# Five small rearrangements in a one-core hybrid encoder block: sums with fewer products, a later scaling, two earlier low parts, a later and cheaper norm

## The chip, the cores and the metric

The kernel runs on one core of one Trainium2 chip. The metric is the device time of one execution in microseconds, taken as the median of three runs of the kernel before; the same kernel was also profiled once, and the profile's rows come from that execution.

## What is computed

The reference is one layer of a residual block over 512 tokens of width 1024. Cut to what matters here:

```python
h = rmsnorm(x); z = h @ W_in                    # 416 latent columns, then diff q, k, v (3 x 512)
x = x + concat([mla(z), diff(z)], -1) @ W_out   # 8 MLA heads of 64, 4 differential heads of 128
h2 = rmsnorm(x)
x = x + (silu(conv3(h2 @ W_gate)) * (h2 @ W_up)) @ W_down      # 2816 wide
x = x + sigmoid(rmsnorm(x) @ W_pg) * (p @ W_pp)

def diff(...):   # per head: two softmaxes, their difference times V, then
    return rms_norm(o, out_g) * (1 - lam_init)
```

So there are three norms of `x` over its 1024 features, and each differential head's output has a norm of its own.

## The kernel before, in words

Everything is float32. Each large product is made of three passes, `mm3` (lines 152 to 157): both operands are split into a high part (rounded to the type `fp32r`, a copy on ScalarE) and a low part (the remainder, a subtraction on VectorE), and TensorE multiplies high by high (L155), high by low (L156) and low by high (L157). So every weight costs a copy on ScalarE and a subtraction on VectorE before its products, and so does every activation. Helpers that do this are `load_w` (L143), `split` (L180), `hi_`, `lo_` and `hl` (L822 to L832).

TensorE holds `x` transposed: 128 features on the partitions, 512 tokens along the free axis, eight such blocks (`xb(b)`). Sums over the features for a norm run over partitions, so TensorE makes them with a matrix of ones.

The order of TensorE's work is written out by hand for the whole kernel. The order of VectorE, ScalarE and GpSimd is written by hand in two stretches (from the start up to the fifth step of the MLA heads, and from the output projection's last part through the first gate and up products); between and behind them the framework's planner draws it up. `tc.issue_after(x)` adds an edge: the instructions in its block are queued behind `x` on the engine of `x`. A tile has a tag, and tiles of one tag share a number of buffers (`bufs`); a load or a copy into a tile waits until its buffer is free.

The parts that the change touches, in order of time:

1. **First norm (L275 to L360).** ScalarE squares the four raw input tiles (two feature blocks of 512 tokens each, side by side), VectorE adds the four into `xq[:, 0]`, 1024 wide (L210, L278). While the latent products `zA` run (`mm3` of 416 columns, four token tiles `t` for each pair of feature blocks `kq`), TensorE sums `xq` over the partitions: for each of four token tiles two products with one column of ones, one for each half of the 1024 (L359). `rms` (L159) turns the sums into `rx`: one VectorE operation and a power on GpSimd (L163). `rx` scales the latent outputs `za` (L367).
2. **MLA heads and the output projection's weights.** `slots` steps through 8 heads by 4 token tiles. The first 512 rows of `w_out` come in four tiles `o00` to `o03` through `load_w`, called when `wo_units` (L638) is first pumped, behind the last MLA step; the three raw buffers and five pairs of high and low buffers are shared with the weights before. `last_mla` (L717) makes, in the last head's steps, the transposes of the finished outputs: `y_split` 0, 1 and 2; `y_split` 3 follows behind the first two steps of the differential heads' logits.
3. **Differential heads (L768 to L786).** `dslots` steps through 4 heads by 4 token tiles; a step makes the logits two steps ahead, pumps units of the output projection (`o`, each ended by VectorE's `add_x`, L631), transposes probabilities, and multiplies by V for the step before (`diff_pv`, L685). At a head's last tile `diff_pv` also makes the output's norm: squares and a copy on ScalarE (L696, L697), a reduction and two small operations on VectorE (L699 to L703), the power on GpSimd (L704), and the scaling of the copy by it on VectorE (L706, 128x512). That call stands in step t = 0 of the next head. Its output is transposed and split in step t = 2 of the next head (`y_split(4 + h - 1)`, L780).
4. **Second norm and the embedding's product (L1008 to L1027).** `norm_r` (L910) sums `nrm["ss"]` with four one-column products, makes the power and spreads it over a diagonal on VectorE (L917); `norm_b` (L919) multiplies ones by that diagonal, and ScalarE copies the result to `nrm["r"]`, 128x512 (L922). `pp_unit(b)`, b = 0 to 7, is one block of the product `p @ W_pp` (six passes, filler for TensorE), `pp_out(b)` its copy on ScalarE into one of three `t5` buffers and its write to DRAM. `tokens` (L978) makes the normed, split inputs `b1` and `b2` of the gate and up products, on VectorE and ScalarE, one block per `next(tk)`.
5. **Gate and up products, first part (L1160 to L1260).** Written out by hand on all engines: three plain products, then products of halves (`gu_units`), with `w_steps` and `token_sums` on VectorE and ScalarE between. `d0 = down_hi(0)` copies the high part of the first down weight, `up_split(2, cv2)` splits the third block's output, `dn0 = [lo_(*d0)]` makes that weight's low part.
6. **Third norm (L1340 to L1350).** After the first half (k = 0 to 3) of the first two blocks of the product `pg`, `norm_r` runs; after the second half `norm_b`. `ple_out` (L1330) multiplies each block by `nrm["r"]` (L1334), which frees its PSUM bank; blocks 0 to 3 use the four banks that blocks 4 to 7 use again.

`rms_v` (L165) is the power by VectorE alone: a first guess from the bits, then three Newton steps, eleven operations in all.

Of the kernel before, what the change touches and what calls it, by code (L numbers as in the profile page):

```python
# [94 lines left out]
def hybrid_block(ctx: ExitStack, tc: tile.TileContext, a: dict, out: bass.AP):  # L95
# [66 lines left out]
        V.tensor_scalar(m, ss, 1.0 / width, EPS, op0=ALU.mult, op1=ALU.add)  # L162
        G.tensor_tensor(y, m, mhalf[:, :n], op=ALU.pow)  # L163

    def rms_v(y, ss, n, width):  # L165

        m, g, t = (sm.tile([P, 32], F32, tag=f"rs_{i}", name=f"rs_{i}")[:, :n] for i in ("n", "g", "t"))
        V.tensor_scalar(m, ss, 1.0 / width, EPS, op0=ALU.mult, op1=ALU.add)
        V.tensor_scalar(y.bitcast(I32), m.bitcast(I32), -0.5, 0x5F3759DF, op0=ALU.mult, op1=ALU.add)
        V.tensor_tensor(g, y, m, op=ALU.mult)  # L170
        for i in range(3):
            V.scalar_tensor_tensor(t, g, -0.5, y, op0=ALU.mult, op1=ALU.mult)
            V.scalar_tensor_tensor(y, t, 1.5, y, op0=ALU.add, op1=ALU.mult)
            if i < 2:
                V.scalar_tensor_tensor(g, t, 1.5, g, op0=ALU.add, op1=ALU.mult)
# [100 lines left out]
    nc.sync.dma_start(mk[QK:100, :], a["maskk"])  # L276
    squares(3)
    V.tensor_tensor(xq[:, 0], xq[:, 0], xq[:, 2], op=ALU.add)  # L278


    rc, rs = {}, {}
# [65 lines left out]
    for kq in range(4):  # L347
        if kq == 0:
            for j in range(2):
                for t in range(NT):  # L350
                    mm3(zps[t][:, :416], xblocks(0, 2, t, *wa[0], 416)[j:j + 1], j == 0, False)
        for t in range(NT):
            if kq:
                mm3(zps[t][:, :416], xblocks(2 * kq, 2 * kq + 2, t, *wa[kq], 416), False, kq == 3)
            if (kq, t) == (2, NT - 1):
                sps = bank("ob", "ssx")
                for u in range(NT):
                    for j in range(2):
                        TE.matmul(sps[:, u:u + 1], xq[:, 0, j * T + u * P:j * T + u * P + P], ones[:, :1], start=j == 0, stop=j == 1)  # L359
                rms(rx, sps[:, :NT], NT, D)  # L360


# [245 lines left out]
        strips.append(strip)  # L608


    yh, yl = [None] * 8, [None] * 8

    def y_split(i, src, col, tag):

        ps = bank(tag, f"yT{i}")
        for t in range(NT):
            TE.transpose(ps[:, tsl[t]], src[:, tsl[t]], ident)
        yh[i], yl[i] = th_tile(f"yh{i}")
        split(yh[i], yl[i], ps, col)

    def wo_blocks(k0, k1, b, w):

# [7 lines left out]
    def add_x(b, ps):  # L630
        V.tensor_tensor(xb(b), xb(b), ps, op=ALU.add)  # L631

    wo2 = {}

    def wo_w(kq, dq):
        return load_w(a["w_out"][kq, dq], 1024, f"o{kq}{dq}")

    def wo_units(kq, dqs, nk):  # L638

        for dq in dqs:  # L640
# [3 lines left out]
            for b in (2 * dq, 2 * dq + 1):  # L644
                ps = bank("acc", f"o{kq}{b}")
                for k in range(0, nk, 2):
# [1 line left out]
                    if k == nk - 2:  # L648
                        add_x(b, ps)
                    yield  # L650

    df = {}

    def diff_T(h, c):
        ps = bank("tp" if h else "acc", f"d{c}T{h}")
        for t in range(NT):
            TE.transpose(ps[:, tsl[t]], zd[c][t][:, h * P:(h + 1) * P], ident)
        h_, l_ = st[4 * (h % 2) + 2 * c], st[4 * (h % 2) + 2 * c + 1]
        split(h_, l_, ps, dcol if c == 0 else None)
        df["qk", h, c] = (h_, l_)  # L660
# [24 lines left out]
    def diff_pv(h, t):  # L685
        if t == 0:
            df["po"] = bank("ob", f"do{h}")
        po, pt = df["po"], df.pop(("pt", h, t))
        for j in range(t + 1):
            TE.matmul(po[:, tsl[t]], pt[:, tsl[j]], zd[2][j][:, h * P:(h + 1) * P], start=j == 0, stop=j == t)  # L690
        if t < NT - 1:
            return
        s0 = df["s0", h]
        yn = tt(f"yd{h}")
        sq = sq_tile("sqo")[:, :T]
        S.activation(sq, po, AF.Square)  # L696
        df["copy"] = S.copy(yn, po)  # L697
        sso = sm.tile([P, NT], F32, tag="sso", name="sso")
        V.reduce_sum(sso, sq.rearrange("p (t d) -> p t d", d=P), axis=AX.X)  # L699

        mo, ro = sm.tile([P, NT], F32, tag="mo", name="mo"), sm.tile([P, NT], F32, tag="ro", name="ro")
        V.scalar_tensor_tensor(mo, s0, EPS, s0, op0=ALU.mult, op1=ALU.mult)
        V.scalar_tensor_tensor(mo, sso, 1.0 / P, mo, op0=ALU.mult, op1=ALU.add)  # L703
        G.tensor_tensor(ro, mo, mhalf[:, :NT], op=ALU.pow)  # L704
        yv = yn.rearrange("p (t d) -> p t d", d=P)
        df["scale"] = V.tensor_tensor(yv, yv, ro.unsqueeze(2).broadcast_to([P, NT, P]), op=ALU.mult)  # L706
        df["y", h] = yn

    dslots = [(h, t) for h in range(DH) for t in range(NT)]
    x_sb = []  # L710
# [19 lines left out]
    for i, (h, t) in enumerate(slots):  # L730
        if i < 2:
            (mla_q, mla_k)[t](1)
        if i + 1 < len(slots):
            mla_logits(*slots[i + 1])
        if i == 4:
            region.__exit__(None, None, None)
            held = tc.issue_after(mla["nm"].ins)
            held.__enter__()
        if i == 8:
            held.__exit__(None, None, None)  # L740
            with tc.issue_after(mla["k"].ins):
                zd_norm(0)
        if 0 < h < H - 1 and t < 2:
            (mla_q, mla_k)[t](h + 1)
        if i == 1:
            lo(*z1_hi(3))
        if i in (9, 11, 13, 15):
            with tc.issue_after(mla["nm"].ins):
                zw2.append(load_w(a["w_d"][2, len(zw2)], 1024, f"d2{len(zw2)}"))
        if h < H - 1:  # L750
            pump(FILL_MLA[t])
        if i == 6:
            bias_strip()
        if h == H - 1:
            if t == 0:
                pump(100)
                fill.append(wo_units(0, range(4), 4))
            last_mla[t]()
        mla["pt", h, t] = probs_T(mla.pop(("pm", h, t)), t, f"m{h}{t}", t % 2)
        if i:  # L760
            mla_pv(*slots[i - 1])
# [6 lines left out]
    for i, (h, t) in enumerate(dslots):  # L768
        if i + 2 < len(dslots):
            diff_logits(*dslots[i + 2])  # L770
        pump(FILL_DIFF[h][t])
        df["pt", h, t] = probs_T(df.pop(("pm", h, t)), t, f"d{h}{t}", True)
        if i:
            diff_pv(*dslots[i - 1])
        if h + 1 < DH and t == 0:
            diff_T(h + 1, 0)
        if t == 3 and h + 2 < DH:
            diff_T(h + 2, 1)
        if h and t == 2:
            y_split(4 + h - 1, df["y", h - 1], ocol, "tp")  # L780
        if h and t == 3:
            if h == 2:
                fill.append(wo_units(1, range(2), 2))
# [223 lines left out]

    tk, w1 = tokens(), w_plain(1)  # L1008
    s0 = hi_(raw_w(gu(0, 2, 4), "rS", 0, bufs=3), "wS", 0)
    for b in range(2):  # L1010
        pp_unit(b)
    norm_r()
    for b in range(2):
        pp_out(b)
    for b in range(2, 4):
        pp_unit(b)
    W[0][1] = lo_(*s0)
    pp_out(2)
# [2 lines left out]
    next(tk)  # L1021
    pp_out(3)
    for b in range(4, 8):
        pp_unit(b)
        next(tk)
        pp_out(b)
    for _ in tk:  # L1027
# [184 lines left out]
    up_mul(cv2, u2, 1.0)  # L1212
    next(new)
    next(g)
    up_split(2, cv2)
    dn0 = [lo_(*d0)]
    w5 = w_steps(5)
    old, g = g, new
    next(g)
# [121 lines left out]
    for k in (0, 4):  # L1341
        for b in range(2):
            pg(b, ps[b], k, k + 4)
        if k == 0:
            norm_r()
    norm_b()
    pg(2, ps[2])
    for b in range(2):
        ple_out(b, ps[b])
# [91 lines left out]
```

## Time and profile before

| | us |
|---|---|
| runs of the kernel before | 655.7, 655.98, 654.2 |
| median | 655.7 |
| profiled execution, its own time | 653.42 |
| its span, first to last instruction | 651.6 |
| TensorE busy in it | 641.6 |
| VectorE busy | 475.2 |
| ScalarE busy | 362.9 |
| GpSimd busy | 56.6 |

The granted TensorE clock was 1.0 throughout. The profiled execution has 1.8 us outside its span, and is 2.3 us below the median. An "idle before" in a timeline row, in brackets, is the time the engine stood still before that instruction and what ended it; the chain of waits is followed back from the last instruction.

### The profile page before, as it was taken

The numbers are of one execution on the slowest core, as the hardware profiler recorded it, in microseconds if no ns is written. First come the engines' busy times: TensorE is split into PE (matmuls) and PEld (weight loads), VectorE is DVE, ScalarE is ACT, GpSimd is POOL, SyncE is SP. The second block draws the span as 40 slices with busy tenths as digits, with TensorE's granted clock in tenths as the row PEclk, the third lists the DMA queues.
The fourth block names the chain that finished last, engine by engine and source line by source line (L and its number), as shares of the span: only waits on it lengthen the run. The fifth ranks groups of instructions, "written<-read, shape, count | busy, mean of one in ns | idle before, by whom it ended". The sixth has DMA issues, their size and how long they took to land.

```text
span 651.6 us, 10276 instructions
## 1 busy us (share of the span) xinstructions
PE 641.6 (98%) x3932; PEld 569.5 (87%) x3932; DVE 475.2 (73%) x860; ACT 362.9 (56%) x631; POOL 56.6 (9%) x93
## 2 busy tenths in 40 slices
PE   9999999999999999999999999999999999999997
PEld 9988888888777778889999999999999999988886
DVE  6789587656878677888886767677767676759444
ACT  7797666457666455556554555455454545637211
POOL 1520040000000121000100000000010000000000
PEclk9999999999999999999999999999999999999999
DMA  8241235234100248636675646565646453531121
GB/s 303 96 162 40 91 73 171 66 115 144 33 33 2 64 179 254 162 70 178 174 215 127 179 114 181 122 197 116 179 114 177 116 176 114 179 130 60 38 80 49
DMA packets 29912, 82.63 MB, mean 127 GB/s; under 512 B 3100, under 2 KB 4124, under 8 KB 29736
## 3 DMA queue, kind: packets, MB, share of 16 engines
q1 hardware_dynamic: 23816, 69.17, 31.9%
q0 software_dynamic: 5616, 12.33, 11.1%
q8 instruction: 31, 0.51, 0.3%
q10 hardware_dynamic: 432, 0.49, 0.2%
q14 instruction: 17, 0.14, 0.1%
HBM read 77.77 MB, written 5.52 MB: 128 GB/s over the span
## 4 chain that ended last, share of the span: by engine, by line
PE 88%; DVE 7%; ACT 3%; issue 1%; DMA 1%; POOL 0%; ACTq 0%; DVEq 0%; POOLq 0%
PE dn L157 6%; PE dn L156 6%; PE dn L155 6%; PE gx L157 4%; PE gx L155 4%; PE gx L156 4%; PE g L155 4%; PE g L156 4%; PE g L157 4%; PE zd L155 3%; PE zd L157 3%; PE zd L156 3%; PE pg L155 2%; PE pg L157 2%; PE pg L156 2%; PE u L155 2%
## 5 line engine op out<-in xcount | busy, mean ns | idle before, releaser
L828 DVE TENSOR_TENSOR wSl<-rS,wSh 128x1024 fp32r<-128x1024 f32 x21 | 25.7, 1224 | 44.5 <-ACT wSh L824 44.4
L157 PE MATMUL dn<-ah,lo_dn 128*128 128x512 f32 x144 | 56.4, 392 | 0.0
L156 PE MATMUL dn<-al,hi_dn 128*128 128x512 f32 x144 | 56.3, 391 | 0.0
L155 PE MATMUL dn<-ah,hi_dn 128*128 128x512 f32 x144 | 56.0, 389 | 0.0
L945 POOL DMA_DIRECT2D rS<-in_w_gu x19 | 22.7, 1195 | 250.9 <-DVE cv L1112 115.0
L824 ACT CAST wSh<-rS 128x1024 fp32r<-128x1024 f32 x21 | 22.1, 1051 | 35.8 <-PE gy L156 35.5
L155 PE MATMUL zd<-hi_d,xh 128*128 128x512 f32 x96 | 39.4, 410 | 0.0
L156 PE MATMUL zd<-lo_d,xh 128*128 128x512 f32 x96 | 37.5, 391 | 0.0
L631 DVE TENSOR_TENSOR x<-x,dn 128x512 f32<-128x512 f32 x44 | 29.8, 678 | 6.5 <-PE dn L157 6.3
L828 DVE TENSOR_TENSOR wTl<-rA,wTh 128x1024 fp32r<-128x1024 f32 x19 | 23.3, 1224 | 14.9 <-ACT wTh L824 14.3
L573 ACT ACTIVATE pm<-ml,nm,rq 128x128 f32<-128x128 f32 (+3 forms) x32 | 19.7, 617 | 22.7 <-DVE nm L571 22.7
L157 PEld LDWEIGHTS dn<-ah,lo_dn 128*128 128x128 f32 x144 | 27.0, 187 | 5.7
L155 PEld LDWEIGHTS dn<-ah,hi_dn 128*128 128x128 f32 x144 | 27.1, 188 | 5.2
L156 PEld LDWEIGHTS dn<-al,hi_dn 128*128 128x128 f32 x144 | 27.0, 188 | 5.3
L155 PE MATMUL o<-yh,hi_o 128*128 128x512 f32 x64 | 26.9, 420 | 1.0 <-DVE x L631 1.0
L1115 ACT ACTIVATE cv<-cv 128x512 f32<-128x512 f32 x22 | 13.9, 631 | 24.5 <-DVE cv L1112 24.4
L824 ACT CAST wAh<-rA 128x1024 fp32r<-128x1024 f32 x21 | 22.0, 1050 | 9.1 <-DMA rA<-in_w_gu 9.1
L570 DVE TENSOR_REDUCE nm<-ml 128x1 f32<-128x128 f32 (+3 forms) x32 | 15.6, 486 | 15.3 <-PE ml L157 15.3
L155 PE MATMUL g<-b2h,wAh 128*128 128x256 f32 (+1 forms) x88 | 26.3, 299 | 0.1
L676 ACT ACTIVATE pmd<-pmd,nmd 128x128 f32<-128x128 f32 (+3 forms) x32 | 17.9, 560 | 15.1 <-DVE nmd L675 15.1
L156 PE MATMUL g<-b2l,wAh 128*128 128x256 f32 (+1 forms) x88 | 26.2, 297 | 0.0
L157 PE MATMUL g<-b2h,wAl 128*128 128x256 f32 (+1 forms) x88 | 26.2, 297 | 0.0
(467 smaller groups left out, 2226.8 us busy)
## 6 DMA issues: line engine op xcount, KB each, us to landing
rA<-in_w_gu SPq DMA_DIRECT2D x22, 512.0 KB, 3.9
rS<-in_w_gu SPq DMA_DIRECT2D x22, 512.0 KB, 3.5
rS<-in_w_gu POOLq DMA_DIRECT2D x19, 512.0 KB, 6.0
raw_dn<-in_w_down SPq DMA_DIRECT2D x18, 512.0 KB, 5.9
raw_d<-in_w_d SPq DMA_DIRECT2D x12, 512.0 KB, 3.7
r<-in_w_gu SPq DMA_DIRECT2D x19, 256.0 KB, 6.5
raw_o<-in_w_out SPq DMA_DIRECT2D x8, 512.0 KB, 3.7
rS_pg<-in_w_pg SPq DMA_DIRECT2D x6, 512.0 KB, 3.9
```

Of the source, the lines that this page charges most:

```text
L155: TE.matmul(ps, xh, wh, start=first and i == 0, stop=False, skip_group_check=again)
L156: TE.matmul(ps, xh, wl, start=False, stop=False, skip_group_check=again)
L157: TE.matmul(ps, xl, wh, start=False, stop=last and i == n - 1, skip_group_check=again)
L570: V.reduce_max(nm, ps[:, :n], axis=AX.X, negate=True)
L573: S.activation(pm[:, :n], ps[:, :n], AF.Exp, bias=nm, scale=r, accum_out=mla["ssum", h // 2][:, t, h % 2:h % 2 + 1])
L631: V.tensor_tensor(xb(b), xb(b), ps, op=ALU.add)
L676: S.activation(pm[:, :n], pm[:, :n], AF.Exp, bias=nm, scale=-1.0, accum_out=s0 if m == 0 else s1)
L824: S.copy(h_, src)
L828: V.tensor_tensor(l_, src, _f32(h_), op=ALU.subtract)
L945: nc.gpsimd.dma_start(sums[f].rearrange("p (i c) -> p i c", i=2), a["w_gu"][f][:, :2048].rearrange("p (i c) -> p i c", i=2)[:, :, :512], a ...
L1115: S.activation(cv, cv, AF.Silu)
```

## The change

The edits: in the first norm the two halves of `xq` are added on VectorE and the sums take four products, one position later; a differential head's scaling (not the last head's) is issued in step t = 1 of the next head; the first output weight is loaded beside the last MLA step, and its low part is queued behind the low part of the third `y_split`; three `pp_unit`s stand ahead of `norm_r` and one more ahead of `norm_b`; the first down weight's low part stands ahead of `up_split(2)`; and the third norm is one product of a matrix of ones with `nrm["ss"]` (128x512) and `rms_v` on all 512 columns, in place of `norm_r` and `norm_b`, its scratch in tiles that are free there.

```diff
-    def rms_v(y, ss, n, width):
-
-        m, g, t = (sm.tile([P, 32], F32, tag=f"rs_{i}", name=f"rs_{i}")[:, :n] for i in ("n", "g", "t"))
+    def rms_v(y, ss, n, width, room=None):
+
+        m, g, t = room or (sm.tile([P, 32], F32, tag=f"rs_{i}", name=f"rs_{i}")[:, :n] for i in ("n", "g", "t"))
...
     V.tensor_tensor(xq[:, 0], xq[:, 0], xq[:, 2], op=ALU.add)
+    V.tensor_tensor(xq[:, 0, :T], xq[:, 0, :T], xq[:, 0, T:], op=ALU.add)
...
-            if (kq, t) == (2, NT - 1):
+            if (kq, t) == (3, 0):
                 sps = bank("ob", "ssx")
                 for u in range(NT):
-                    for j in range(2):
-                        TE.matmul(sps[:, u:u + 1], xq[:, 0, j * T + u * P:j * T + u * P + P], ones[:, :1], start=j == 0, stop=j == 1)
+                    TE.matmul(sps[:, u:u + 1], xq[:, 0, tsl[u]], ones[:, :1], start=True, stop=True)
                 rms(rx, sps[:, :NT], NT, D)
...
-        split(yh[i], yl[i], ps, col)
+        df["ysplit"] = split(yh[i], yl[i], ps, col)
...
-    wo2 = {}
+    wo2, wo_first = {}, {}
 
     def wo_w(kq, dq):
+        if (kq, dq) in wo_first:
+            return wo_first.pop((kq, dq))
         return load_w(a["w_out"][kq, dq], 1024, f"o{kq}{dq}")
...
         yv = yn.rearrange("p (t d) -> p t d", d=P)
-        df["scale"] = V.tensor_tensor(yv, yv, ro.unsqueeze(2).broadcast_to([P, NT, P]), op=ALU.mult)
         df["y", h] = yn
+        df["scaling"] = lambda: V.tensor_tensor(yv, yv, ro.unsqueeze(2).broadcast_to([P, NT, P]), op=ALU.mult)
+        if h == DH - 1:
+            df["scale"] = df["scaling"]()
...
             last_mla[t]()
+            if t == NT - 1:
+                raw = load_raw(a["w_out"][0, 0], 1024, "o00")
+                hi_o, lo_o = (wts.tile([P, 1024], F32R, tag=i, bufs=NW, name=f"{i}_o00") for i in ("hi", "lo"))
+                S.copy(hi_o, raw)
+                with tc.issue_after(df["ysplit"].ins):
+                    V.tensor_tensor(lo_o, raw, _f32(hi_o), op=ALU.subtract)
+                wo_first[0, 0] = (hi_o, lo_o)
...
+        if h and t == 1:
+            df["scaling"]()
...
-    for b in range(2):
+    for b in range(3):
         pp_unit(b)
     norm_r()
     for b in range(2):
         pp_out(b)
-    for b in range(2, 4):
+    for b in range(3, 5):
         pp_unit(b)
...
     for b in range(4, 8):
-        pp_unit(b)
+        if b < 7:
+            pp_unit(b + 1)
         next(tk)
         pp_out(b)
...
+    dn0 = [lo_(*d0)]
     up_split(2, cv2)
-    dn0 = [lo_(*d0)]
...
         if k == 0:
-            norm_r()
-    norm_b()
+            sps = bank("ob", "nr3")
+            TE.matmul(sps, ones, nrm["ss"], start=True, stop=True)
+            rms_v(nrm["r"], sps, T, D, (nrm["dg"], nr_[1][:, T:], nrm["ss"]))
```

More of the change, by code (lines that the diff above doesn't have):

```diff
@@ L608, in bias_strip @@
         strips.append(strip)
-    yh, yl = [None] * 8, [None] * 8
+    yh, yl, df = [None] * 8, [None] * 8, {}
     def y_split(i, src, col, tag):
@@ L650, in wo_units @@
                     yield
-    df = {}
     def diff_T(h, c):
```

## The prediction, made before the changed kernel ran

> **What bounds the kernel now.** I read the page first, then the chain of waits, then the view of who waited for whom on TensorE, and last the timeline around each wait.
>
> ```profile
> PE 641.6 (98%) x3932; PEld 569.5 (87%) x3932; DVE 475.2 (73%) x860; ACT 362.9 (56%) x631; POOL 56.6 (9%) x93
> PE 88%; DVE 7%; ACT 3%; issue 1%; DMA 1%; POOL 0%; ACTq 0%; DVEq 0%; POOLq 0%
> L155 PE MATMUL o<-yh,hi_o 128*128 128x512 f32 x64 | 26.9, 420 | 1.0 <-DVE x L631 1.0
> ```
>
> TensorE is busy for 98% of the span and carries 88% of the chain. Time can be won in two ways only: TensorE does less, or one of its few waits goes. Those of more than a moment, apart from the start's, are these (us in total, times, longest):
>
> ```profile
> PE pTm L538 <- ACT pm L573: 1.1, 2, 0.9
> PE o L155 <- DVE x L631: 1.0, 1, 1.0
> PE gx L157 <- DVE wAl L828: 0.6, 1, 0.6
> PE kT L557 <- DVE st L187: 0.5, 2, 0.2
> PE dl L157 <- DVE st L187: 0.4, 1, 0.4
> PE nr L914 <- DVE nr L886: 0.4, 1, 0.4
> ```
>
> They add to 4.0 us. A record of a 512-column product is about 0.42 long (row above) and the next starts 0.23 later (607.88 row below), so records overlap by some 0.16 and a wait behind such a product costs TensorE up to 0.16 more than its row.
>
> **Products that go.**
>
> ```profile
> 20.27 1.68 PE ssx L359 x16
> 606.75 0.79 PE nr L914 x8
> 607.54 0.35 PE pg L155
> 607.88 0.23 PE pg L156
> 613.14 0.86 PE nrb L921 x2
> ```
>
> The first norm's eight one-column products show as 16 passes in 1.68 us, 0.105 each; four products go, 8 passes, **0.84 us** off TensorE's path. Before them VectorE gets one more addition of 128x512; the next fence has one at 0.69. Two things cover it: the sums now stand six 416-column products later, and if that were too little, what is left of the 0.69 would fall on TensorE.
>
> At the third norm the eight passes take 0.79, and the product behind them 0.35 in place of 0.23: 0.91 us. The spreading product, 0.86, stays in another form: ones by `ss`, again 512 float32 columns. So **0.91 us** goes. The power and the diagonal give way to eleven VectorE operations of 512 columns. No such chain is in the trace; its nearest row is a 128x512 operation on two tensors:
>
> ```profile
> 614.66 0.69 DVE L1334 TENSOR_TENSOR sg<-pg,nr 128x512 f32<-128x512 f32 x1 [5.08 <-ACT nr L922]
> 624.96 0.69 DVE L1334 TENSOR_TENSOR sg<-pg,nr 128x512 f32<-128x512 f32 x1 [1.50 <-PE pg L157]
> ```
>
> Eleven by 0.69 is 7.6 us. They start at the end of the new product, about 606.75 + 0.86 = 607.6, and end at about 615.2; the first user is at 614.66 now. So the first `ple_out` runs half a microsecond later. Who waits: block 4's product, which takes block 0's bank. Blocks 2 and 3 still lie ahead of it, 48 passes of 0.23 from 614.0 on, so it starts at 625.0 now and at 624.1 then. The cover is over 8 us, and I cost the eleven operations at nothing; they fall on the path only if they take twice their estimate.
>
> **The first output weight's low part.** The MLA heads hold one wait on VectorE that comes from it:
>
> ```profile
> 115.26 1.14 DVE lo_o L149
> 119.13 0.67 DVE st L187
> ```
>
> The low part of `o00` ran at 115.26, though its first use is behind the MLA heads; the split `st` ended 0.05 before `kT` (the row `PE kT`) could start. Without 1.14 ahead of it that wait goes: half of the row's 0.5, plus the overlap, **0.4 us**. No other low part can move into its place, since the next needs a pair of buffers that the differential values' weights still hold. The load on SyncE's queue and the high part keep their places, as far as buffers decide; the raw buffer is held some 45 us longer, so the later loads of `w_out` make do with two, each still issued a low part ahead of the one that uses it.
>
> Now the low part runs behind the third output's:
>
> ```profile
> 161.52 0.29 DVE L675 CUSTOM_DVE_ANT_0 pmd<-dl,strip 128x128 f32<-128x128 f32 x1 [0.43 <-PE dl L157]
> 162.47 0.69 DVE L588 TENSOR_TENSOR ym<-mo,rcp 128x512 f32<-128x512 f32 x1 [0.44 <-PE mo L583]
> 166.74 0.61 DVE yh3l L184
> 167.40 0.50 PE o L156
> ```
>
> VectorE stands still there for 0.43 and 0.44, which takes in 0.87 of 1.14. The rest, 0.27, is queued ahead of the fourth output's low part, and the product at 167.40 starts 0.05 after that ends: bounds 0 and 0.35; I take **0.2 us lost**, near the rest.
>
> **The heads' scaling.**
>
> ```profile
> 201.34 1.01 POOL L704 TENSOR_TENSOR ro<-mo,mhalf 128x4 f32<-128x4 f32 x1 [14.57 <-DVE mo L703]
> 201.79 0.61 DVE L682 SCALAR_TENSOR_TENSOR pmd<-pmd,cf 128x384 f32<-128x384 f32 x1
> 202.38 0.69 DVE L706 TENSOR_TENSOR yd<-yd,ro 128x512 f32<-128x512 f32 x1
> 214.49 0.62 DVE pmd L682
> 216.52 1.02 POOL ro L704
> 217.56 0.69 DVE L706 TENSOR_TENSOR yd<-yd,ro 128x512 f32<-128x512 f32 x1 [0.58 <-POOL ro L704]
> 218.26 0.61 DVE x L631
> 218.91 0.50 PE o L155
> ```
>
> Before the last head's step VectorE stands for 0.58 until the power ends at 217.54, scales, and only then adds the `x` whose bank TensorE waits for: the 1.0 row. With the scaling a step later the addition can start at 217.0, 1.2 us sooner, which is more than the wait: **1.1 us** with the overlap. In the head before, the scaling at 202.38 stands directly ahead of the split that `dl` waits for: 0.69 sooner ends the whole wait, **0.45 us**. The scaling costs the same wherever it runs; its user is the transpose in step 2, a step of TensorE work behind, so I cost its new place at nothing.
>
> A rule of the Trainium skill speaks against this (SBUF — State Buffer, section Who interferes with whom): a VectorE instruction with two inputs in SBUF contends with a GpSimd instruction that reads SBUF, and the second to start stands still until the first ends. By it VectorE, freed of its wait, would stand still anyway under the power. The rows do not bear it out: the combination at 201.79 began 0.45 into the power and took 0.61, as the same one at 214.49 did with no power beside it (0.62).
>
> **The second norm, and what happens to its gain.** With `pp_unit(2)`, six passes, ahead of `norm_r` the `nr` wait of 0.4 (0.5 with the overlap) goes. But the norm then starts when those passes end, 6 by 0.23 less the 0.5 later: about 0.85. TensorE has won 0.5, and the chain from the norm to `tokens` is 0.85 late. Is there slack?
>
> ```profile
> 248.00:258.60 10.60, 10.60 (x47) 8.40 (x46) 8.79 (x14) 5.75 (x11) 0.00 (x0) 1.00 1.02 306
> 258.68 0.59 ACT L937 COPY ppo<-pp 128x512 f32<-128x512 f32 x1 [0.80 <-DMA pps<-ppo]
> DVE wTl L828 <- ACT wTh L824: 2.0, 2, 1.7
> DVE wSl L828 <- ACT wSh L824: 1.1, 1, 1.1
> DVE b2l L987 <- ACT b2h L989: 0.5, 1, 0.5
> DVE wAl L828 <- ACT wAh L824: 0.5, 1, 0.5
> ```
>
> The last four rows are all waits of VectorE from 259 to 291.7, where `gx` waits for `wAl`. None is ended by TensorE: VectorE and ScalarE hand each other casts and low parts all the way from the `ppo` copy at 258.68, which a DMA released. So the time at 291 is set by that DMA, not by TensorE, and the 0.5 won is waited away there. The DMA is in a stretch where the engines are full (share 1.02, 306 GB/s): it starts up to 0.85 later but carries one 256 KB write less, since `ppo` 2 now goes out before it, worth 0.86 at that rate. Bounds 0 and 0.85 late; nearest to 0 by the rate, I take 0.2 **lost**.
>
> The first down weight's low part then acts on the next wait of the same chain:
>
> ```profile
> 301.18 0.69 DVE L184 TENSOR_TENSOR al<-cv,ah 128x512 fp32r<-128x512 f32 x1 [1.02 <-ACT ah L183]
> 301.79 1.22 DVE L828 TENSOR_TENSOR lo_dn<-raw_dn,hi_dn 128x1024 fp32r<-128x1024 f32 x1
> 301.35 1.04 ACT L824 CAST wAh<-rA 128x1024 fp32r<-128x1024 f32 x1
> ```
>
> VectorE idles 1.02 before `al`. Put there, `lo_dn` delays `al` by 0.2, and `wAl`, which ran behind `lo_dn`, starts when its high part ends, at 302.4 instead of about 302.9 (`lo_dn` ends at 303.0 and records overlap a little here too): `gx` gets **0.5 us** back. Together 0.3 won.
>
> **The sum.** 0.84 + 0.91 + 0.4 - 0.2 + 1.1 + 0.45 + 0.3 = 3.8 us. The profiled execution took 653.42 (span 651.6, 1.8 around it); it would take 649.6. The median of the runs is 2.3 above it; taken from that, 655.7 - 3.8 = **651.9 us**, 0.6% less. Of this, 1.75 are passes that are gone and need no wait to vanish.
>
> **The rivals.**
>
> *The scaling keeps its place.* VectorE's order there is the planner's. If it deals the scaling as soon as it counts the power as done, it stands ahead of the addition as now, or so late that the transpose waits 0.7 for it. For: the planner put it there before, idle time and all. Against: its place in the program is now behind that addition. The 1.55 are lost: 653.4. By the Trainium skill's rule the time would be this too, the 1.55 being stood out under the power.
>
> *The chain pays in full.* The write does not shorten the full stretch: 0.85 late instead of 0.2, so 652.5. For: `ppo` 3 to 5 are also issued later. Against: the rate.
>
> *A new dealing of low parts: slower.* One row shows what a low part in the wrong place does:
>
> ```profile
> 155.52 1.21 DVE L149 TENSOR_TENSOR lo_o<-raw_o,hi_o 128x1024 fp32r<-128x1024 f32 x1
> ```
>
> It ran just ahead of the last small step of a row maximum; the exponential followed, and `pTm` waited 0.9 (1.07 with the overlap). A moved step lets the planner deal VectorE's list anew from the MLA heads on. Twelve low parts lie there, and two cost TensorE something now. From the fourth more in such a place on, the kernel is slower; five give 5 x 1.07 - 3.8 = +1.5, 657.2. Against: the edits there are small and late.
>
> **How the numbers follow.** Forecast 0.60; scaling keeps its place 0.17; the Trainium skill's rule 0.03; the chain pays in full 0.13; new dealing 0.07. A measurement of this kernel tells about 0.3%, 2.0 us, from no change. The forecast and the chain rival lie beyond it nearly always, 0.72; the two cases at 653.4 in six of ten, 0.12: faster 0.84. Of the rest, 0.08 from those and 0.03 of the others fall within: same 0.11. Slower 0.05. The low end adds what could go beyond: the 0.2 of the MLA heads, and in the second norm's chain the 0.5 kept, the 0.2 not lost and the last 0.1 of the `gx` row, 1.0 in all, and half a microsecond because the runs of before spread over 1.8: 650.4. The high end is the scaling rival with the chain paid in full, 0.65 more, and a little of the `yh3l` bound: 654.2.
>
> **What would show it.** Right: L359 with 8 passes at 0.84 and no `nr` passes near 607; no wait `o <- x` over 0.3 and none of `dl` on `st`; L706 in the second and third head behind an addition, with no idle before it; the wait `nr <- nr` gone, `gx` waiting longer at 291 and less at 303; eleven operations of 0.7 near 608 with TensorE not waiting behind them. Wrong: a `yT` that waits for `yd`, a wait of `pg` on `sg` near 624, several new waits of `pTm`, `pTd` or `dl` between 76 and 235, or low parts dealt in other places there.

## The result and the profile after

| | before | after |
|---|---|---|
| median, us | 654.59 (5 runs, 653.7 to 655.98) | 650.83 (5 runs, 649.71 to 651.4) |
| profiled execution, us | 653.42 | 649.71 |
| its span, us | 651.6 | 647.9 |

The ratio is 0.9937 (95% interval 0.9921 to 0.9954): 3.8 us less by the medians, 3.7 by the two spans; the forecast was 3.8. The forecast time, 651.9, is 1.1 above the measured one because the median of before fell by 1.1 with two more runs.

The page of after, its lines of busy time and of the chain that ended last:

```profile
PE 639.4 (99%) x3916; PEld 567.8 (88%) x3916; DVE 481.3 (74%) x870; ACT 361.8 (56%) x630; POOL 55.5 (9%) x92
...
PE 91%; DVE 5%; ACT 3%; issue 1%; ACTq 0%
```

TensorE has 16 records fewer and carries 91% of the chain. What TensorE waited for in after (us in total, times, longest):

```profile
...
PE o L155 <- ACT yh L183: 0.6, 1, 0.6
PE pTm L538 <- ACT pm L573: 0.5, 2, 0.3
PE g L155 <- ACT ppo L948: 0.5, 1, 0.5
PE o L156 <- DVE yh3l L184: 0.4, 1, 0.4
PE kT L557 <- DVE st L187: 0.2, 1, 0.2
```

Four of the six waits of before are gone (`o <- x`, `gx <- wAl`, `dl <- st`, `nr <- nr`), two are halved. Three are new: `o <- yh`, `o <- yh3l`, and `g <- ppo`, the first gate product waiting for ScalarE's copy of an embedding block. The prediction had only the one on `yh3l`, at 0.2 (at most 0.35).

To see where the time went I cut each span at three products: the first of `zd`, the first of `g` (first gate product) and the first of `dn` (first down product). This is the view of windows, first before, then after; the columns are the window, its length, then the busy time of TensorE, its weight loads, VectorE, ScalarE and GpSimd, and the clock, DMA share and GB/s:

```profile
26.45:254.27 227.82, 224.25 (x1304) 188.34 (x1302) 171.48 (x428) 144.49 (x304) 26.97 (x58) 1.00 0.30 94
254.27:310.21 55.94, 55.21 (x326) 48.73 (x325) 46.30 (x69) 32.67 (x51) 3.70 (x4) 1.00 0.56 154
310.21:651.60 341.39, 336.78 (x2172) 307.39 (x2170) 238.19 (x326) 163.82 (x243) 18.77 (x16) 1.00 0.49 135
```

```profile
25.80:251.56 225.76, 223.31 (x1304) 188.11 (x1303) 171.02 (x435) 144.55 (x305) 28.26 (x62) 1.00 0.29 95
251.56:307.45 55.89, 55.55 (x324) 48.85 (x325) 47.00 (x71) 33.34 (x51) 3.56 (x3) 1.00 0.55 157
307.45:647.90 340.45, 335.83 (x2164) 306.62 (x2162) 244.72 (x335) 163.07 (x242) 17.88 (x15) 1.00 0.48 136
```

The start won 26.45 - 25.80 = 0.65 us, the heads and the norm 2.06, the chain behind the norm 0.05, the rest with the third norm 0.94. For the first, second and last the prediction had 0.84, about 2.25 (0.4 - 0.2 + 1.55 + 0.5), and 0.91; the third, where it had 0.2 lost net, came out even. How far each of these numbers comes from the terms that were predicted is taken up further down.

The same cuts through every experiment, from the starts of the same three rows and the span:

| run | first `zd` at | to first `g` | to first `dn` | to the end |
|---|---|---|---|---|
| before | 26.45 | 227.82 | 55.94 | 341.39 |
| s1_sums | 25.46 | 227.90 | 55.87 | 341.47 |
| s2_scaling | 26.39 | 225.36 | 57.15 | 341.40 |
| s3_lowpart | 26.43 | 227.39 | 56.19 | 341.39 |
| s4_norm3 | 26.39 | 227.86 | 56.31 | 340.44 |
| after | 25.80 | 225.76 | 55.89 | 340.45 |
| u_pp | 25.73 | 226.79 | 55.50 | 340.48 |
| u_low | 26.42 | 225.66 | 55.99 | 340.53 |
| i1_pp | 25.21 | 224.89 | 55.23 | 340.47 |
| i2_low | 25.33 | 225.70 | 56.10 | 340.47 |
| i3_both | 25.38 | 224.55 | 55.23 | 340.44 |
| i4_ppfree | 27.38 | 225.46 | 55.21 | 340.45 |

The last column has only two values, 341.4 and 340.45 (the spans are rounded to a tenth), so a tenth counts there. In the others, runs whose program is the same up to the cut show what doesn't count: s4_norm3 differs from before only at the third norm and has 0.37 more in the third column; from after to i4_ppfree seven runs have the same start and `zd` from 25.21 to 27.38.

### The profile page after: what moved, and what is told of

It is laid out like the page before. It is cut to its first block, busy times and chain, and to the rows that moved or that the text cites. A ratio compares the mean times of both kernels' runs of the same rounds, so it can differ in the third digit from the quotient of the medians.

```text
span 647.9 us, 10246 instructions
## 1 busy us (share of the span) xinstructions
PE 639.4 (99%) x3916; PEld 567.8 (88%) x3916; DVE 481.3 (74%) x870; ACT 361.8 (56%) x630; POOL 55.5 (9%) x92
## 4 chain that ended last, share of the span: by engine, by line
PE 91%; DVE 5%; ACT 3%; issue 1%; ACTq 0%
PE dn L157 6%; PE dn L156 6%; PE dn L155 6%; PE gx L157 4%; PE gx L155 4%; PE gx L156 4%; PE zd L155 3%; PE zd L157 3%; PE zd L156 3%; PE g L155 3%; PE g L156 3%; PE g L157 3%; PE o L155 3%; PE mo L583 2%; PE o L156 2%; PE pg L157 2%
## 5 line engine op out<-in xcount | busy, mean ns | idle before, releaser
L839 DVE TENSOR_TENSOR wTl<-rA,wTh 128x1024 fp32r<-128x1024 f32 x19 | 23.3, 1225 | 15.0 <-ACT wTh L835 14.5
L839 DVE TENSOR_TENSOR wAl<-rA,wAh 128x1024 fp32r<-128x1024 f32 x21 | 25.6, 1217 | 1.2 <-ACT wAh L835 1.2
```

The source lines that it names most:

```text
L839: V.tensor_tensor(l_, src, _f32(h_), op=ALU.subtract)
```

## One part of the change alone

These four ran once each; before took 654.91 on that chip, once as well. I read them by the table.

**s1_sums: before with the first norm's sums alone.**

```diff
+    V.tensor_tensor(xq[:, 0, :T], xq[:, 0, :T], xq[:, 0, T:], op=ALU.add)
...
-            if (kq, t) == (2, NT - 1):
+            if (kq, t) == (3, 0):
...
-                    for j in range(2):
-                        TE.matmul(sps[:, u:u + 1], xq[:, 0, j * T + u * P:j * T + u * P + P], ones[:, :1], start=j == 0, stop=j == 1)
+                    TE.matmul(sps[:, u:u + 1], xq[:, 0, tsl[u]], ones[:, :1], start=True, stop=True)
```

> The kernel before with the first norm's edit alone (one addition more, four one-column products in place of eight, one position later). Theory as in the prediction: 8 passes less, 0.84 us, the addition is covered; the first zd product starts 0.84 sooner against the last zA product of before, and the profiled time falls by 0.8. Rival, read from the changed kernel's trace: the addition lies on VectorE ahead of the lambda's small operations and of rms, so rx comes 0.7 later, ScalarE's first za copy ends after TensorE is done with zA, and the first zd product waits for it: 0.6 to 0.7 won, with zd starting within 0.1 of the end of the first za copy.

652.47 us. The first `zd` starts 0.99 earlier and every later column stays: the passes are won and kept, and `zd` waits for nothing. The start of a run also depends on when its first loads land; counted from the last `zA` product ahead of the old place of the sums (19.92 in before) `zd` comes 0.89 sooner, and in after 0.82, where 0.84 was predicted. In the chain of waits of after the sums are half of what they were (1.68 for 16 before):

```profile
21.58 0.85 PE ssx L359 x8
```

**s2_scaling: before with the later scaling alone.**

```diff
-        df["scale"] = V.tensor_tensor(yv, yv, ro.unsqueeze(2).broadcast_to([P, NT, P]), op=ALU.mult)
+        df["scaling"] = lambda: V.tensor_tensor(yv, yv, ro.unsqueeze(2).broadcast_to([P, NT, P]), op=ALU.mult)
+        if h == DH - 1:
+            df["scale"] = df["scaling"]()
...
+        if h and t == 1:
+            df["scaling"]()
```

> The kernel before with the later scaling alone. Theory: the waits o <- x (1.0) and dl <- st (0.4) go, nothing waits for the scaled output, VectorE no longer stands still for the power in the heads 1 to 3; TensorE's place at the end of the heads is 1.5 to 1.7 us earlier, the profiled time falls by as much. Rival 1: the planner puts the scaling where it was, nothing changes. Rival 2 (the rule on GpSimd's and VectorE's shared port): VectorE's two-input operations under the power stretch by up to 1 us and the waits stay.

652.12 us. The waits `o <- x` and `dl <- st` are gone; by the distance of starts they had cost 1.13 and 0.53, 1.66 in all, against 1.55 in the prediction. The second column is shorter by 2.46, so another 0.8 is in no term of the prediction. By the shift of TensorE's rows against before, 0.46 of it arises between 180 and 203 us, in differences of about a tenth each (0.12 ahead, then 0.58); s1_sums and s4_norm3, which are equal to before there, move by 0.04 at most. There VectorE in before had stood still for the power ahead of a scaling once more, in a head for which the prediction has no term:

```profile
186.80 0.69 DVE L706 TENSOR_TENSOR yd<-yd,ro 128x512 f32<-128x512 f32 x1 [0.49 <-POOL ro L704]
```

That the 0.46 is this idle time is likely, not shown: s3_lowpart, without the later scaling, gains 0.5 in the same stretch, though it enters it 0.3 late. VectorE's timeline in after shows the order that was forecast: the addition to `x` first, then the scaling (L707), in the last head and with no idle before it. (In the head before, at 202.22, the scaling has no idle either; it stands behind the split `st` but ahead of the addition.)

```profile
215.39 0.68 DVE L631 TENSOR_TENSOR x<-x,o 128x512 f32<-128x512 f32 x1
216.05 0.69 DVE L707 TENSOR_TENSOR yd<-yd,ro 128x512 f32<-128x512 f32 x1
```

In this run half of the gain is given back in the third column, 57.15 for 55.94. ScalarE's timeline shows where: first before, then s2_scaling. The copies `ppo` take turns with three buffers and wait until a write to DRAM has given one back.

```profile
256.78 0.59 ACT L937 COPY ppo<-pp 128x512 f32<-128x512 f32 x1 [2.46 <-DMA pps<-ppo]
...
258.68 0.59 ACT L937 COPY ppo<-pp 128x512 f32<-128x512 f32 x1 [0.80 <-DMA pps<-ppo]
```

```profile
255.46 0.59 ACT L941 COPY ppo<-pp 128x512 f32<-128x512 f32 x1 [3.66 <-DMA pps<-ppo]
...
257.35 0.59 ACT L941 COPY ppo<-pp 128x512 f32<-128x512 f32 x1 [0.78 <-DMA pps<-ppo]
```

TensorE reached this stretch 2.5 us sooner, the write came back only 1.3 sooner: 3.66 - 2.46 = 1.20 more of waiting, which is the 1.21 of the column. From the last copy to the first `dn` it takes the same time in both: 310.21 - 258.68 = 51.53 and 308.90 - 257.35 = 51.55.

An earlier start alone does not do this. The view of DMA from 249 to 254 us has the writes with their time to landing, in before, s2_scaling and u_pp (a run further down, which has the later scaling and the same order of copies):

```profile
pps<-ppo SPq DMA_DIRECT2D x3, 256.0 KB, 6.0
```

```profile
pps<-ppo SPq DMA_DIRECT2D x3, 256.0 KB, 7.2
```

```profile
pps<-ppo SPq DMA_DIRECT2D x3, 256.0 KB, 6.1
```

The write took 1.2 longer in s2_scaling, and the load `raw_dn` beside it 7.1 where before has 6.0. In u_pp TensorE comes 1.75 sooner than in before, the copy waits 2.47 as it does in before, and the gain passes whole. So the loss belongs to this one execution, as far as the runs show; why its transfers were slower stays open.

**s3_lowpart: before with the pinned low part of `o00` alone.**

```diff
+            if t == NT - 1:
+                raw = load_raw(a["w_out"][0, 0], 1024, "o00")
+                hi_o, lo_o = (wts.tile([P, 1024], F32R, tag=i, bufs=NW, name=f"{i}_o00") for i in ("hi", "lo"))
+                S.copy(hi_o, raw)
+                with tc.issue_after(df["ysplit"].ins):
+                    V.tensor_tensor(lo_o, raw, _f32(hi_o), op=ALU.subtract)
+                wo_first[0, 0] = (hi_o, lo_o)
```

> The kernel before with the first output weight's load and pinned low part alone. Theory from the changed kernel's trace: the pinned low part keeps back all later low parts of w_out, since their tiles are dealt in turn; none runs between 116 and 158, five run in the 12 us behind the pinned one, and the fourth output's high and low parts wait behind them. Won: 0.4 at kT (119) and 0.5 at pTm (157); lost: 1.1 to 1.3 at the o products near 167; together 0 to 0.5 us lost. Rival, the prediction: the other low parts keep their places (137, 143, 149, 155), only 1.14 of work moves, 0.4 won and 0.2 lost, pTm's 0.9 stays.

653.25 us. Its waits near 157 and 166 us are those of after to 0.1, and the reason is on VectorE's timeline of after, where before had low parts of `w_out` at 115, 137, 144, 149 and 155 us:

```profile
158.38 0.69 DVE L184 TENSOR_TENSOR yh2l<-yT,yh 128x512 fp32r<-128x512 f32 x1
158.98 1.22 DVE L766 TENSOR_TENSOR lo_o<-raw_o,hi_o 128x1024 fp32r<-128x1024 f32 x1
...
160.65 1.18 DVE L149 TENSOR_TENSOR lo_o<-raw_o,hi_o 128x1024 fp32r<-128x1024 f32 x1
...
165.07 1.22 DVE L149 TENSOR_TENSOR lo_o<-raw_o,hi_o 128x1024 fp32r<-128x1024 f32 x1
166.28 0.67 DVE L184 TENSOR_TENSOR yh3l<-yT,yh 128x512 fp32r<-128x512 f32 x1
167.00 1.22 DVE L149 TENSOR_TENSOR lo_o<-raw_o,hi_o 128x1024 fp32r<-128x1024 f32 x1
...
169.60 1.22 DVE L149 TENSOR_TENSOR lo_o<-raw_o,hi_o 128x1024 fp32r<-128x1024 f32 x1
```

All the others ran behind the pinned low part (158.98), four of them within 12 us, in the very stretch in which `o` uses them. For the fourth weight and the later ones the trace shows why: each of the three raw buffers comes free with a low part, so SyncE issues the fourth load at 160.26, when the pinned one has ended (158.98 + 1.22 = 160.20), where before had issued five loads by 139. The second and third had their high parts by 142 and were held back all the same; that buffers of one tag are dealt in turn would explain it, but no run shows that alone. The new order takes the low part at 155.5 out of `pTm`'s way (by distance of starts 1.07 before, 0.50 after) and the one at 115 out of `kT`'s (0.4), and puts others in front of `yh3l`; and ScalarE's high part of the fourth weight, waiting for its late load, holds up `yh`:

```profile
164.00 1.05 ACT L148 CAST hi_o<-raw_o 128x1024 fp32r<-128x1024 f32 x1 [0.35 <-DMA raw_o<-in_w_out]
...
165.46 0.56 ACT L183 CAST yh<-yT 128x512 fp32r<-128x512 f32 x1
```

By the shift of TensorE's rows against before, s3_lowpart is 0.42 ahead at 120 us, 1.53 at 158, and 0.17 behind at 167. At the end of the column it is 0.4 ahead, chiefly by the 0.5 between 180 and 203 us named above.

**s4_norm3: before with the third norm alone.**

```diff
         if k == 0:
-            norm_r()
-    norm_b()
+            sps = bank("ob", "nr3")
+            TE.matmul(sps, ones, nrm["ss"], start=True, stop=True)
+            rms_v(nrm["r"], sps, T, D, (nrm["dg"], nr_[1][:, T:], nrm["ss"]))
```

> The kernel before with the third norm's edit alone. Theory: 8 passes less at 607, 0.9 us won at the end; eleven operations of 512 columns take 7 to 8 us on VectorE, the first ple_out starts 0.3 to 0.8 later, TensorE does not wait for block 0's bank. Rival: the operations take over 1.4 us each (two inputs in SBUF, an integer step), the chain lasts over 16 us and block 4's product waits: less than 0.9 won or a loss.

652.81 us. The last column falls from 341.39 to 340.44: 0.95. In after VectorE's operations, ten of 0.69 and one of 0.43, start at 604.89 and end just ahead of the first `ple_out`, and TensorE's list of waits has no `pg`:

```profile
606.08 0.69 DVE L170 TENSOR_TENSOR nr<-nr,nr 128x512 f32<-128x512 f32 x1
...
611.64 0.69 DVE L173 SCALAR_TENSOR_TENSOR nr<-nr,nr 128x512 f32<-128x512 f32 x1
612.44 0.69 DVE L1346 TENSOR_TENSOR sg<-pg,nr 128x512 f32<-128x512 f32 x1
```

## The change with one part taken back

These two, and i1_pp and i2_low below, were timed against a median of 653.83 for before, i3_both and i4_ppfree against 653.47, so it is the ratios that compare with after's 0.9937.

**u_pp: after with the old order of the embedding's units.**

```diff
-    for b in range(3):
+    for b in range(2):
         pp_unit(b)
     norm_r()
...
-    for b in range(3, 5):
+    for b in range(2, 4):
         pp_unit(b)
...
-        if b < 7:
-            pp_unit(b + 1)
+        pp_unit(b)
         next(tk)
```

> The changed kernel with the order of the per-layer products (pp units) put back; all its other parts stay. My theory now: the order wins TensorE's wait for the sums of the second norm (0.52 us before, row nr <- DVE nr) and loses as much again, because the bank of the first gate product is pp5's and its copy now stands between two tokens on ScalarE (wait g <- ACT ppo 0.52). So here the 0.5 before the norm's sums comes back, the 0.5 at the first gate product goes, and first gate product and end stand within 0.3 us of the changed kernel: 650.8, 650.2 to 651.4. The rival, which is what the prediction had: the 0.5 is really won, the norm's sums are late here by 0.5 and nothing gives it back ahead of the chain at 291 us, so that the first gate product starts 0.5 us later than in the changed kernel and the time is 651.3.

650.3 us, ratio 0.9942 (0.9923 to 0.9962): no difference from after that these runs can show. TensorE's waits in it:

```profile
...
PE kT L557 <- DVE st L187: 0.7, 2, 0.5
PE o L155 <- ACT yh L183: 0.7, 1, 0.7
...
PE nr L925 <- DVE nr L897: 0.4, 1, 0.4
```

`nr` waits again, and `g <- ppo` is not in the list: the one wait was exchanged for the other. The second column is 1.03 longer than after's all the same; 0.74 of that arises by `kT` (119 us), where the two programs are equal and VectorE and ScalarE have the same order. So equal programs can differ there by that much.

The third column is 0.39 shorter, which may be the price of the new order. From the end of the norm's last addition to the last `ppo` copy it takes 14.6 us here and in before, 15.0 to 15.3 in after, u_low and i2_low, where the new order stands. The parts alone, which have the old order, take 14.5 to 14.9 but for s2_scaling, whose write was slow (15.7). So the price of 0.4 fits, but single runs do not settle it.

**u_low: after with the low part of `o00` left to the planner** (the edit of s3_lowpart taken back).

> The changed kernel with the low part of the first weights of the output projection left to the planner again. My theory now: the pinned low part keeps back every later one of its tag, so that it is worth nothing: without it the low parts stand at about 115, 137, 144, 149 and 155 us again, TensorE's wait for the transposes near 157 us is 1.07 us again (0.50 in the changed kernel), the waits of o on yh and on yh3l near 166 us (0.79 and 0.71 by distance of starts) are 0.3 together, the heads of the second attention stand within 0.3 us of the changed kernel, and so does the end: 650.8, 650.2 to 651.4. The rival, which is the prediction's term: the edit wins 0.2 us net, kT near 119 us waits 0.4 us again and the time is 651.0, with no more than 0.2 us shorter waits near 166 us. The places of the rows tell the two apart, the time alone does not.

649.85 us, ratio 0.9937 (0.992 to 0.9954): again no difference from after. The rows are where the theory had them: the low parts at 115 to 156 us again, on VectorE,

```profile
115.25 1.22 DVE L149 TENSOR_TENSOR lo_o<-raw_o,hi_o 128x1024 fp32r<-128x1024 f32 x1
...
155.64 1.22 DVE L149 TENSOR_TENSOR lo_o<-raw_o,hi_o 128x1024 fp32r<-128x1024 f32 x1
```

and on TensorE the wait of `pTm` back at 0.9 and those of `o` gone (the one on `yh3l` is 0.3 by distance of starts). The second column is 0.10 shorter than after's.

## What a better version shows

**i1_pp: after with ScalarE's copies out of the tokens' way,** and with the first steps of the token sums (`next(ts[0])`) ahead of the first convolution.

```diff
-    norm_b()
-    next(tk)
-    pp_out(3)
-    for b in range(4, 8):
-        if b < 7:
-            pp_unit(b + 1)
-        next(tk)
-        pp_out(b)
+    for b in range(3, 5):
+        pp_out(b)
+    norm_b()
+    pp_unit(5)
+    pp_out(5)
+    next(tk)
+    for b in range(6, 8):
+        pp_unit(b)
     for _ in tk:
         pass
     next(w1)
+    for b in range(6, 8):
+        pp_out(b)
...
+    next(ts[0])
     cv0 = conv_a(0, g0)
     next(ts[0])
     conv_b(0, g0, cv0)
-    next(ts[0])
```

> The changed kernel with ScalarE's copies of the pp units moved: 3 and 4 go into its idle time ahead of the norm's row, 5 ahead of the first token, 6 and 7 behind all the tokens and behind the second half of the next weights, and the first four subtractions of the token sums go ahead of the first convolution. Nothing is left out. My theory: the chain on VectorE and ScalarE from the tokens to the products of block 3 is started late by the copies that wait for a transfer to give back their buffer (2.18 and 0.80 us of ScalarE's time in the changed kernel), and what happens in that stretch is carried through to the waits at 285 to 304 us. So the last token's low part ends near 258 us instead of 260.2, the first gate product does not wait for its bank (0.5 won), and the waits of g and gx from 285 to 304 us (0.25, 0.20, 0.23, 0.31 by distance of starts) go: 1.0 to 1.5 us, 649.5 (649.2 to 650.2). The rival: the chain is bound by the first gate product's end (262.1 us) and by VectorE's own work behind it, so that only the 0.5 at the bank is won and the waits from 285 to 304 us stay: 650.3.

648.02 us, ratio 0.9908 (0.9893 to 0.9923), 1.9 us less than after by the two ratios, somewhat more than the theory's 1.0 to 1.5. ScalarE's timeline, first after, then i1_pp:

```profile
254.47 0.59 ACT L948 COPY ppo<-pp 128x512 f32<-128x512 f32 x1 [2.18 <-DMA pps<-ppo]
254.95 0.62 ACT L1000 CAST b2h<-xg 128x512 fp32r<-128x512 f32 x1
256.37 0.59 ACT L948 COPY ppo<-pp 128x512 f32<-128x512 f32 x1 [0.80 <-DMA pps<-ppo]
```

```profile
252.67 0.62 ACT L1000 CAST b2h<-xg 128x512 fp32r<-128x512 f32 x1 [0.65 <-DVE xg L996]
...
257.94 1.06 ACT L948 COPY ppo<-pp 128x512 f32<-128x512 f32 x2
```

The casts now wait only for VectorE. The third column is 55.2 in all three runs with this edit, TensorE busy for 55.0 of it; of the waits from 285 to 304 us one of 0.15 is left:

```profile
250.10:305.33 55.23, 55.03 (x326) 48.84 (x324) 48.10 (x72) 33.99 (x52) 3.56 (x3) 1.00 0.59 165
```

That is 0.66 less than after, and with the 0.52 of `g <- ppo` gone, 1.18 of the gain has its place; the earlier start of `zd` (0.59) and the rest are within what equal programs differ by. So the rival, a chain bound by the gate product, falls. The chain was held by a transfer, as the prediction had it, but only through the copies in front of it. The run has two edits, and the second, which puts two low parts `btl` ahead of the first convolution on VectorE, was not run alone. It lies behind the 0.52 and behind the tokens: the last `b2l` ends at 260.24 in after and at 257.81 here, 2.43 sooner, with TensorE only 1.46 sooner at the first `g`. How the 0.66 of the third column is shared between the two edits is not shown.

**i2_low: after with `o00`'s low part left to the planner and the fifth one, `o10`, pinned behind the fourth y's.**

```diff
+        if (kq, dq) == (1, 0):
+            raw = load_raw(a["w_out"][kq, dq], 1024, "o10")
+            hi_o, lo_o = (wts.tile([P, 1024], F32R, tag=i, bufs=NW, name=f"{i}_o10") for i in ("hi", "lo"))
+            S.copy(hi_o, raw)
+            with tc.issue_after(df["y3"].ins):
+                V.tensor_tensor(lo_o, raw, _f32(hi_o), op=ALU.subtract)
+            return hi_o, lo_o
```

> The changed kernel with the first low part of the output projection left to the planner, and the fifth (the first of the second half of the rows, o10) pinned behind the low part of the fourth y instead. Nothing is left out. My theory: TensorE's wait near 157 us (1.07 us before) is that of the fifth low part, which the planner had put at 155.5 us in front of the copy of the transposes, and the waits near 166 us in the changed kernel (0.79 and 0.71 by distance of starts) are those of the low parts kept back. With the fifth pinned and the others free, both are gone: waits near 157 us under 0.5, near 166 us under 0.4 together, the second attention 0.8 to 1.2 us earlier than in the changed kernel; at the end 0.5 to 1.0 us of it is left, 650.1 (649.7 to 650.5). The rival: the copy near 157 us is late for another reason (ScalarE's exponentials, the masks), then the wait of about 1.0 us stays and the time is 650.8.

649.36 us, ratio 0.9935 (0.9915 to 0.9955): no gain. Its waits are as the theory had them, `pTm` at 0.50 and `o` at 0.29 by distance of starts, so the cause of the wait near 157 us is shown: the fifth low part. TensorE was 1.17 ahead of after at 167 us, 0.7 of it won since the first `zd`. But by 203 us all but 0.1 of this was gone. ScalarE's timeline of i2_low near 192 us, and the same row of u_low:

```profile
192.48 1.05 ACT L807 CAST pk<-raw_pp 128x1024 fp32r<-128x1024 f32 x1 [1.54 <-DMA raw_pp<-in_w_pp]
```

```profile
193.30 1.05 ACT L801 CAST pk<-raw_pp 128x1024 fp32r<-128x1024 f32 x1 [0.74 <-DMA raw_pp<-in_w_pp]
```

TensorE was 1.7 ahead of u_low at 186 us, the cast behind the load of `raw_pp` only 0.8, and the exponentials of the heads are queued behind this cast. It fits, but no run moved that load, so for this place the cause is argued only.

**i3_both: i1_pp and i2_low together.**

> The two edits i1_pp and i2_low together, as a version that may beat both kernels; nothing is left out. My theory: i2_low won 0.6 us near 166 us and had lost it again by 203 us, where VectorE's order holds the heads of the second attention, so that nothing of it reaches the norm, and a chain with room behind it cannot carry it on: the time is that of i1_pp within its spread, 0.991 of before (0.989 to 0.993), and the heads stand within 0.2 us of i1_pp's from 203 us on, counted from the start of the zd products. The rival: what i2_low won was eaten only by the chain behind the second norm; with i1_pp's room it comes through, 0.6 us less than i1_pp, 0.990 of before.

648.18 us, ratio 0.9912 (0.9895 to 0.9929): no quicker than i1_pp alone, and the two are the quickest here. From the first `zd` on it is 0.34 ahead of i1_pp at 203 us and 0.34 in the second column: between theory (0.2) and rival (0.6), and within what equal programs differ by.

**i4_ppfree: i1_pp on u_low.**

> The edit i1_pp on the changed kernel without its low-part edit (u_low); nothing is left out. My theory: the low-part edit is worth nothing, between 0.1 us lost and 0.1 won at the end, so the time is that of i1_pp within the spread, 0.991 of before (0.989 to 0.993), with the wait of 1.07 us near 157 us and under 0.4 us of waits near 166 us. The rival, the prediction's term of 0.2 us won by the edit: 0.2 us longer than i1_pp from 203 us on, counted from the start of the zd products.

648.59 us, ratio 0.9921 (0.9901 to 0.9942). Its second column is 0.57 longer than i1_pp's, so here the pinned low part looks like a gain of 0.5, where u_low against after made it a loss of 0.1. i4_ppfree is u_low up to 238 us, yet it lost 0.35 to 0.5 against u_low from 198 to 203 us, behind a `raw_pp` that landed 4.28 us after its issue instead of 3.56. The worth of the edit to `o00` stays open between 0.1 lost and 0.5 won.

## Why the prediction was right, and where it was not

- **Products that go.** 0.84 and 0.91 were predicted. Counted from the same `zA` product the first came to 0.89 alone and 0.82 in after; the second to 0.95 and 0.94. Right. The new addition and the eleven operations cost nothing, as said; the cover held.
- **The scaling.** 1.55 predicted, 1.66 by the two waits that went. Right in place, order and size. (The 0.16 that the prediction adds to a wait is not 0.42 less 0.23, which is 0.19; the two waits bear out 0.17: 1.13 for 0.96 of idle time, 0.53 for 0.36.) A gain of about 0.5 between 180 and 203 us had no term: the prediction looked at two of the three scalings that move, and before had idled ahead of the other one as well. The sum let the gain through to the end whole, and u_pp bears that out; the loss in s2_scaling goes with the slow transfers of that run.
- **The first output weight's low part.** The 0.4 at `kT` came. The step that failed: "the later loads of `w_out` make do with two, each still issued a low part ahead of the one that uses it". All later low parts, and the loads from the fourth on, came behind the pinned one, from 158.98 on. So 1.2 were lost near 166 us where 0.2 (at most 0.35) were allowed, and 0.6 won near 157 us that were not foreseen. With the 0.4 this comes to 0.2 to 0.3 lost by 180 us, where 0.2 won was predicted; by the time of whole runs the edit's worth stays open (0.1 lost to 0.5 won).
- **The second norm.** The 0.5 before `nr` came, but was not "waited away" at 291 us: it went at once, at 251.56, in `g <- ppo`. The bank of the first gate product is that of `pp_unit(5)`, whose copy stands behind a token's cast on ScalarE. The prediction followed the copies' DMA, not the bank they free. The chain came some 0.4 late in after where 0.2 were taken (bounds 0 and 0.85), if u_pp tells it rightly.
- **The down weight's low part.** 0.5 predicted. From the last `ppo` copy to the first `dn` before and the four parts alone take 51.53 to 51.55, after takes 307.45 - 256.37 = 51.08, u_pp and i2_low 51.06 and 51.05: 0.45 to 0.5. Right. With the later chain it makes the 0.05 of the third column.
- **The rivals.** The scaling did not keep its place. The chain paid at most half of the full price. The new dealing did happen, but in two places, not five.

The sum of 3.8 was right to 0.1 partly by luck. By the shift of TensorE's rows, after is 0.57 ahead of before at 115 us, 0.30 at 180 and 0.90 at 203: 0.3 lost at the low parts where 0.2 won was predicted, then 0.6 won that no term had. The start showed 0.65 for 0.84 in this run, by its first loads, and the second norm with the chain gave nothing where 0.3 was predicted.

## What to carry to other kernels

Before pinning one tile's instruction, list all tiles that share its tag, the derived ones too, and the loads that wait for its buffers: here all of them ended up behind it. When a filler is moved, follow the bank it frees and the engine that frees it, not its transfer alone. Where copies wait for a write to give back their buffer, one slow transfer can hold up all behind them (1.2 us in s2_scaling), so keep them out of the way of the work that others wait for: the version that did this took 1.9 us less than after, about half of what the whole change had won, though 1.2 of it alone has its place in the trace.

## What was not expected of the hardware

- The same first instructions took from 25.21 to 27.38 us. In i4_ppfree the second cast of the first weights waited 3.17 for its load, in i1_pp 0.56, with issue times equal to 0.1. These 2.2 us are as much as the times of one kernel spread (1.7 in after); that they are the cause there is not shown, as only one execution of each kernel has a trace. ScalarE's timeline, first i4_ppfree, then i1_pp:

```profile
9.20 0.54 ACT L183 CAST hi_a<-raw_a 128x416 fp32r<-128x416 f32 x1 [3.17 <-DMA raw_a<-in_w_a]
```

```profile
6.74 0.54 ACT L183 CAST hi_a<-raw_a 128x416 fp32r<-128x416 f32 x1 [0.56 <-DMA raw_a<-in_w_a]
```

- VectorE under GpSimd's power, again not slowed. In after the power runs from 199.98 to 200.99; a VectorE instruction with two full-width inputs starts 0.44 into it and takes 0.62:

```profile
199.98 1.01 POOL L704 TENSOR_TENSOR ro<-mo,mhalf 128x4 f32<-128x4 f32 x1 [14.06 <-DVE mo L703]
```

```profile
200.42 0.62 DVE L682 SCALAR_TENSOR_TENSOR pmd<-pmd,cf 128x384 f32<-128x384 f32 x1
```

  By the Trainium skill (SBUF — State Buffer, Who interferes with whom) it should have stood still until the power ended; the trace does not agree, as far as GpSimd's spans, which are rough, can tell. The rule is for two inputs in SBUF, as this instruction has them. The addition to `x` reads one of its two from PSUM, so that the rule would not have held it up, and the prediction's rival by it did not follow for the 1.1.
